# A block-causal mask in the softmax instead of in the products, and three moves around it

## The chip, the cores and the metric

The kernel runs on one core of one Trainium2 chip. The metric is the time of one execution in microseconds, as the device reports it; lower is better. Abbreviations as in the profile: PE is TensorE's matrix multiplication, PEld its weight load, ACT is ScalarE, DVE is VectorE, POOL is GpSimd, SP is SyncE, which here only issues DMAs.

## What is computed

An encoder trunk of two layers on 256 rows of 1024 columns, all in float32. Layer 0 is feed-forward, convolution, feed-forward; layer 1 is feed-forward, attention, feed-forward. The change touches the attention (8 heads; 128 columns of a query or key without rotation, 64 with it; chunks of 64 rows):

```python
chunk_id = jnp.arange(seq) // CHUNK                    # CHUNK = 64, seq = 256
for blk in range(seq // Q_BLOCK):                      # Q_BLOCK = 128
    q0, q1 = blk * Q_BLOCK, (blk + 1) * Q_BLOCK
    s = (jnp.einsum("bqhd,bkhd->bhqk", q_nope[:, q0:q1], k_nope[:, :q1], ...)
         + jnp.einsum("bqhr,bkr->bhqk", q_rope[:, q0:q1], k_rope[:, :q1], ...)) * scale
    mask = chunk_id[q0:q1, None] >= chunk_id[None, :q1]
    s = jnp.where(mask[None, None], s, -jnp.inf)
    p = jax.nn.softmax(s, axis=-1).astype(v.dtype)
    outs.append(jnp.einsum("bhqk,bkhd->bqhd", p, v[:, :q1]))
o = jnp.concatenate(outs, axis=1)
return o.reshape(o.shape[0], seq, N_HEADS * V_HEAD) @ w_o
```

A row sees its own chunk and the chunks before it. Of a block of 128 query rows the upper 64 therefore do not see the last 64 of the block's key columns, and the lower 64 see all of them.

## The kernel before, in words

All large products are made from two parts of each operand, a rounded high part and the rest, as three products (`mm3`, lines 269, 272 and 273). Weights come in blocks of 1 MB: SP's DMA into a `raw` tile (3 buffers), a cast to the high part on ACT (line 185), and the low part on DVE (line 186), each in two pieces, into `hi` and `lo` tiles (5 buffers). `load_to(n)` records the casts of all blocks up to number n; `load_ahead(k)` does so up to k blocks beyond the one in use.

A scheduler that works on the recorded program sets the final order of each engine. It follows the order of recording and the data, but instructions recorded under `urgent` have priority, and `order(a, b)` makes a follow b. `urgent` also keeps the last instructions of what it ran, and the casts recorded later are put behind these (`behind`).

The attention's products up to keys and values come first (`nope`, the copies at lines 1212 and 1257). The last weights of the queries, those of heads 4 to 7, are used after the first scores. Then, per head:

- `scores`: for each of two query blocks `qb`, a float32 product of the unrotated parts (line 1267), one of the rotated parts (line 1268), and a bfloat16 product of one row of ones with one row of -1e30 (line 1269), which adds -1e30 at the upper 64 rows and last 64 columns. Both blocks of a head, 128 and 256 columns, lie in one bank of the tag "B", of which there are 3.
- `softmax`: on DVE the maximum of each block (line 1279) and its scaling (line 1280); on ACT Exp with the sum of its row (line 1282, followed by a read of the accumulator); on DVE the reciprocal (line 1284) and the scaled probabilities (line 1286).
- `probs`: three transposes on PE (line 313, the same banks "B"), and a copy of the result, `ptT`, on ACT (line 1292).
- `values`: two float32 products with the values (lines 1301 and 1302), in one bank of the tag "C"; `evicted` copies the result to a high part `Oh` on ACT (line 1296) and a low part `Ol` on DVE (line 1297).
- the output projection, `Rows`: one block of weights for every two heads, 24 products of 512 columns.

The loop over `i` runs these staggered: the scores of head i, the transposes of head i-2, the values of head i-3, and at i = 6 and i = 8 a block of the projection. The other two blocks come in `finish`, which then adds to the residual rows and begins the next norm.

Of the kernel before, what the change touches and what calls it, by code (L numbers as in the profile page):

```python
# [11 lines left out]
F32 = mybir.dt.float32  # L12
F32R = mybir.dt.float32r
BF16 = mybir.dt.bfloat16
I32 = mybir.dt.int32
AF = mybir.ActivationFunctionType
ALU = mybir.AluOpType
AX = mybir.AxisListType

P = 128  # L20
D = 1024
S = 256
NT = S // P
# [4 lines left out]
CHUNK = 64  # L28
# [3 lines left out]
H = 8  # L32
# [10 lines left out]
PIECES = 2  # L43
# [16 lines left out]
SCALE = float((NOPE + ROPE) ** -0.5)  # L60
# [22 lines left out]
def trunk(ctx: ExitStack, tc: tile.TileContext, x, xt, pos, invf, gains, gfin, wdw,  # L83
          f1w13, f1w2, f2w13, f2w2, cw1, cw2, wa, wuq, wukv, wo, wpair, out):
    nc = tc.nc

    const = ctx.enter_context(tc.tile_pool(name="const", bufs=1))
# [4 lines left out]
    small = ctx.enter_context(tc.tile_pool(name="small", bufs=4))  # L92
# [5 lines left out]
    def uid(s):  # L98
        n_uid[0] += 1
        return f"{s}_{n_uid[0]}"  # L100
# [4 lines left out]
    def bank(tag, name):  # L105
        return ps.tile([P, 512], F32, tag=tag, name=uid(name), bufs=BANKS[tag])
# [23 lines left out]
    loaded = []  # L130
    n_used = [0]
# [3 lines left out]
    def order(ins, first):  # L135
        tc.add_manual_dep(ins.ins, first.name, mybir.DependencyInfo(
            mybir.DependencyClass.NoSync, mybir.DependencyReason.DATA), reason="order")
# [7 lines left out]
    casts = {}  # L145
# [13 lines left out]
    def load(src, pieces=1):  # L159
        if isinstance(src, tuple):  # L160
            raw = rawp.tile([P, HB], F32, tag="raw", name=uid("raw"))
            nc.sync.dma_start(raw, src[1])
            return raw
        n = src.shape[-1]
        there = len(loaded) in raws
        raw = raws.pop(len(loaded))[0] if there else rawp.tile([P, HB], F32, tag="raw", name=uid("raw"))
        hi = wp.tile([P, HB], F32R, tag="hi", name=uid("hi"))
        lo = wp.tile([P, HB], F32R, tag="lo", name=uid("lo"))
        if there:
            pass  # L170
        elif len(loaded) < 7:

            for i in range(pieces if len(loaded) < 4 else 1):
                c = slice(i * n // pieces, (i + 1) * n // pieces) if len(loaded) < 4 else slice(n)
                fetch(raw[:, c], src[:, c])
        else:
            dma = nc.sync.dma_start(raw[:, :n], src)
            if turns:

                order(dma, turns[-1].ins)  # L180
        for i in range(pieces):
            c = slice(i * n // pieces, (i + 1) * n // pieces)

            low = nc.gpsimd if len(loaded) == conv_block[-4] else nc.vector
            casts[len(loaded), i] = (nc.scalar.copy(hi[:, c], raw[:, c]),  # L185
                                     low.tensor_sub(lo[:, c], raw[:, c], hi[:, c].bitcast(F32)))  # L186
            for cast in casts[len(loaded), i]:
                behind(cast)
        return hi, lo
# [14 lines left out]
    def load_ahead(ahead=W_BUFS - 2):  # L204
        load_to(min(len(blocks), n_used[0] + ahead))

    def load_to(last):
        while len(loaded) < last:
            loaded.append(load(blocks[len(loaded)], PIECES))
# [29 lines left out]
    for k in range(KT):  # L239
        c = slice(k % 4 * 512, k % 4 * 512 + 512)  # L240
# [6 lines left out]
    neghalf = const.tile([P, 1], F32, name="neghalf")  # L247
# [19 lines left out]
    def mm3(o, ah, al, bh, bl, start, stop, after=()):  # L267

        mm = nc.tensor.matmul(o, ah, bl, start=start, stop=False)  # L269
        for a in after:  # L270
            order(mm, a.ins)
        nc.tensor.matmul(o, ah, bh, start=False, stop=False)  # L272
        return nc.tensor.matmul(o, al, bh, start=False, stop=stop)  # L273
# [8 lines left out]
    def tbs(tb):  # L282
        return slice(tb * P, (tb + 1) * P)
# [831 lines left out]
    def mla_in(act, X, make_next, cc, sn):  # L1115
        R = X.r
        CQ = act.tile([P, H, S], F32R, tag="CQ", name="CQ")
        CQh, CQl = CQ[:, :4, :], CQ[:, 4:, :]
# [4 lines left out]
        KR = act.tile([P, 2, S], F32, tag="KR", name="KR")  # L1123
        nc.gpsimd.memset(KR, 0.0)

        mq = const.tile([P, P], BF16, name="mq")
        nc.gpsimd.memset(mq, 0.0)
        nc.gpsimd.memset(mq[0:1, :CHUNK], 1.0)
        mk = const.tile([P, CHUNK], BF16, name="mk")
        nc.gpsimd.memset(mk, 0.0)  # L1130
        nc.gpsimd.memset(mk[0:1, :], -1e30)

        last_low = [None]

# [39 lines left out]
        last = None  # L1174
        for tb in range(NT):
# [5 lines left out]
            last = last_low[0]  # L1181
# [15 lines left out]
        QR = act.tile([P, 4, S], F32, tag="QR", name="QR")  # L1197
        KN = xp.tile([P, H, S], F32, tag="Xh", name="KN")
        QN = xp.tile([P, H, S], F32, tag="Xl", name="QN")
        VV = act.tile([P, NT, H * VH], F32, tag="VV", name="VV")  # L1200

        def nope(part, dst, nk, ch, cl, width, h0, heads, after=()):

            hi, lo = part
            for i in range(heads[0], heads[1], 2):
                b = bank("A", "nope")
                for e in range(2):
                    for k in range(nk):
                        c = slice(k * width + (i + e) * P, k * width + (i + e + 1) * P)
                        mm = mm3(b[:, e * S:(e + 1) * S], hi[:, c], lo[:, c], ch[:, k, :], cl[:, k, :],  # L1210
                                 k == 0, k == nk - 1, after if k == 0 else ())
                nc.scalar.copy(dst[:, h0 + i:h0 + i + 2, :], b.rearrange("p (e t) -> p e t", t=S))
            return mm
# [4 lines left out]
        for tb in range(NT):  # L1218
            u = bank("A", "qr")
            qu.append(u)  # L1220
            for k in range(4):
                after = (last,) if k == 0 else turned if (tb, k) == (0, 2) else ()
                last = mm3(u, CQh[:, k, tbs(tb)], CQl[:, k, tbs(tb)], hi[:, k * 512:(k + 1) * 512],
                           lo[:, k * 512:(k + 1) * 512], k == 0, k == 3, after)
# [13 lines left out]
        part, = weights()  # L1238
        last = nope(part, QN, 4, CQh, CQl, 512, 0, (0, 4), turned)
        for t in range(NT):  # L1240
            b = transposed(kd[t], 0, 1, (last,))
# [3 lines left out]
        for tb in range(NT):  # L1245
            b = transposed(qr[tb], 0, 4, (last,))
# [4 lines left out]
        for tb in range(NT):  # L1251
            for d in range(2):
                b = bank("A", "v")
                for k in range(2):
                    c = slice(k * D + d * 512, k * D + d * 512 + 512)
# [6 lines left out]
        def scores(hd):  # L1262
            b = bank("B", "sc")
            sc = {0: b[:, :P], 1: b[:, P:P + S]}
            for qb in range(NT):
                n = (qb + 1) * P
                nc.tensor.matmul(sc[qb], QN[:, hd, tbs(qb)], KN[:, hd, :n], start=True, stop=False)
                nc.tensor.matmul(sc[qb], QR[:, hd // 2, tbs(qb)], KR[:, hd % 2, :n], start=False, stop=False)
                nc.tensor.matmul(sc[qb][:, n - CHUNK:n], mq, mk, start=False, stop=True)
            return softmax(sc)  # L1270

        @urgent
        def softmax(sc):
            nm = small.tile([P, NT], F32, tag="nm", name=uid("nm"))
            sm = small.tile([P, NT], F32, tag="sm", name=uid("sm"))
            pr = act.tile([P, 3 * P], F32, tag="pr", name=uid("pr"), bufs=3)
            pn = {0: pr[:, :P], 1: pr[:, P:]}
            for qb in range(NT):
                nc.vector.reduce_max(nm[:, qb:qb + 1], sc[qb], axis=AX.X)
            nc.vector.tensor_scalar(nm, nm, -SCALE, None, op0=ALU.mult)  # L1280
            for qb in range(NT):
                nc.scalar.activation(pn[qb], sc[qb], AF.Exp, scale=SCALE, bias=nm[:, qb:qb + 1],
                                     accum_out=sm[:, qb:qb + 1])
            nc.vector.reciprocal(sm, sm)
            for qb in range(NT):
                nc.vector.tensor_scalar(pn[qb], pn[qb], sm[:, qb:qb + 1], None, op0=ALU.mult)
            return pr

        def probs(pr):
            b = transposed(pr, 0, 3)  # L1290
            pt = act.tile([P, 3 * P], F32, tag="ptT", name=uid("ptT"), bufs=2)
            nc.scalar.copy(pt, b[:, :3 * P])
            return pt
# [5 lines left out]
        def values(hd, pt):  # L1299
            b = bank("C", "pv")  # L1300
            nc.tensor.matmul(b[:, :S], VV[:, 0, hd * VH:(hd + 1) * VH], pt[:, :S], start=True, stop=False)
            nc.tensor.matmul(b[:, P:S], VV[:, 1, hd * VH:(hd + 1) * VH], pt[:, S:], start=False, stop=True)

            (urgent if hd in (3, 4) else lambda f: f)(evicted)(hd, b)

        pr, pt = {}, {}
        part, = weights()
        load_ahead(4)
        pr[0] = scores(0)
        nope(part, QN, 4, CQh, CQl, 512, 4, (0, 2))  # L1310
        pr[1] = scores(1)
        nope(part, QN, 4, CQh, CQl, 512, 4, (2, 4))
        o = Rows(Oh, Ol, H)
        for i in range(2, H + 3):
            if i < H:
                pr[i] = scores(i)
            if i == 6:
                load_ahead(5)
            if i - 2 < H:
                pt[i - 2] = probs(pr[i - 2])  # L1320
            if i - 3 in pt:
                values(i - 3, pt[i - 3])
            if i in (6, 8):
                o.block((i - 6) // 2)
        return o.finish(None, make_next, act)

    dw = const.tile([P, KT, TAPS], F32, name="dw")
# [137 lines left out]
```

## Time and profile before

| | |
|---|---|
| median of 3 runs | 923.6 us (923.42 to 923.61) |
| the profiled execution's own time | 923.93 us |
| its span (first to last instruction) | 922.1 us |
| granted TensorE clock | 0.999 of full speed |
| busy: PE, DVE, ACT, POOL | 911.7, 591.3, 494.6, 123.8 us |
| the attention from its first scores to the next norm's first transposes | 685.7 to 735 us of the span |

A row of the profile by time has the start, the time from the first start to the last end, the engine, the line, the operation with the tiles it writes and reads, and how many it merges; in square brackets, how long the engine sat idle before it and what ended that. Instructions overlap at their ends, so what an instruction costs its engine is the time from its start to the next start, not its length. A float32 product is two rows, since PE makes two passes of it. A group's row (line, engine, operation, shapes, count) has the busy time, the mean length in ns, and the idle time before.

### The profile page before, as it was taken

The page shows a single profiled execution, that of the slowest core. Times are in us where ns is not written, and L with a number is a line of the kernel's source. Part 1 is how long each engine was busy: PE and PEld are TensorE (multiplying, and loading weights), DVE is VectorE, ACT ScalarE, POOL GpSimd, SP SyncE. Part 2 cuts the span into 40 slices and gives each one's busy share as a digit, 9 for nine tenths or more (in the row PEclk, how much of TensorE's full clock was granted, in tenths as well). Part 3 has the DMA queues.
Part 4 walks back from the last instruction along what each step waited for, and adds up shares of the span by engine and source line. Part 5 has one row for each costly group of instructions (what it writes and reads, how often), then busy time and mean ns, then how long its engine had stood idle before and what let it go on. Part 6 is the DMA issues. An engine that isn't in the chain of part 4 may idle for free.

```text
span 922.1 us, 12110 instructions
## 1 busy us (share of the span) xinstructions
PE 911.7 (99%) x4348; PEld 764.8 (83%) x4348; DVE 591.3 (64%) x931; ACT 494.6 (54%) x844; POOL 123.8 (13%) x255
## 2 busy tenths in 40 slices
PE   9999999999999999999999999999999999999997
PEld 7888888898978888888888888888898788888886
DVE  6886664489987666664476665545785586556633
ACT  7655453488877444553365444533685474454422
POOL 1730000079942000000010000000200000000000
PEclk9999999999999999999999999999999999999999
DMA  9887775534217766775567776753471377677611
GB/s 332 313 300 254 279 250 220 183 138 137 93 61 272 261 229 234 252 253 197 183 223 265 245 245 233 253 187 132 171 278 50 138 260 275 234 244 261 224 46 46
DMA packets 65293, 194.73 MB, mean 211 GB/s; under 512 B 11857, under 2 KB 37073, under 8 KB 45905
## 3 DMA queue, kind: packets, MB, share of 16 engines
q1 hardware_dynamic: 64656, 193.27, 60.1%
q8 instruction: 34, 0.56, 0.2%
q10 hardware_dynamic: 576, 0.69, 0.2%
q14 instruction: 27, 0.21, 0.1%
HBM read 179.78 MB, written 14.16 MB: 210 GB/s over the span
## 4 chain that ended last, share of the span: by engine, by line
PE 96%; ACT 2%; DVE 1%; DMA 0%; issue 0%; POOL 0%; POOLq 0%; ACTq 0%; DVEq 0%
PE u L269 17%; PE u L272 17%; PE u L273 17%; PE o L269 9%; PE o L272 9%; PE o L273 9%; PE gate L744 3%; PE u L744 3%; PE o L993 1%; PE u L278 1%; PE tp L313 1%; PE pairs L787 1%; PE a L273 1%; PE a L269 1%; PE a L272 1%; PE nope L269 1%
## 5 line engine op out<-in xcount | busy, mean ns | idle before, releaser
L186 DVE TENSOR_TENSOR lo<-raw,hi 128x1024 fp32r<-128x1024 f32 (+1 forms) x292 | 344.4, 1220 | 187.4 <-ACT hi L185 186.8
L185 ACT CAST hi<-raw 128x1024 fp32r<-128x1024 f32 x294 | 292.8, 1048 | 254.8 <-PE o L273 89.6
L269 PE MATMUL u<-lo,Xh 128*128 128x512 f32 x688 | 267.9, 389 | 0.0
L273 PE MATMUL u<-hi,Xl 128*128 128x512 f32 x688 | 267.8, 389 | 0.0
L272 PE MATMUL u<-hi,Xh 128*128 128x512 f32 x688 | 267.7, 389 | 0.0
L273 PEld LDWEIGHTS u<-hi,Xl 128*128 128x128 f32 x688 | 129.2, 188 | 27.3 <-DVE Xl L332 0.4
L269 PEld LDWEIGHTS u<-lo,Xh 128*128 128x128 f32 x688 | 129.2, 188 | 27.2 <-DVE lo L186 0.4
L272 PEld LDWEIGHTS u<-hi,Xh 128*128 128x128 f32 x688 | 129.2, 188 | 26.6
L272 PE MATMUL o<-hi,Gh 128*128 128x512 f32 (+1 forms) x356 | 137.9, 387 | 0.0
L273 PE MATMUL o<-hi,Gl 128*128 128x512 f32 (+1 forms) x356 | 137.8, 387 | 0.0
L269 PE MATMUL o<-lo,Gh 128*128 128x512 f32 (+1 forms) x356 | 137.2, 387 | 0.0
L304 POOL TENSOR_TENSOR ms<-ss 128x1 f32<-128x1 f32 x16 | 8.0, 504 | 597.7 <-ACT junk L296 597.7
L269 PEld LDWEIGHTS o<-lo,Gh 128*128 128x128 f32 x356 | 66.9, 188 | 13.6
L273 PEld LDWEIGHTS o<-hi,Gl 128*128 128x128 f32 x356 | 66.9, 188 | 13.5
L272 PEld LDWEIGHTS o<-hi,Gh 128*128 128x128 f32 x356 | 66.9, 188 | 13.3
L637 DVE TENSOR_TENSOR Gl<-gb,Gh 128x512 fp32r<-128x512 f32 (+1 forms) x48 | 31.4, 653 | 48.1 <-ACT Gh L636 48.1
L636 ACT CAST Gh<-gb 128x512 fp32r<-128x512 f32 (+1 forms) x48 | 28.0, 583 | 60.5 <-DMA gb<-gd 60.5
L821 DVE SCALAR_TENSOR_TENSOR acc<-V,dw,acc 128x128 f32<-128x128 f32 (+1 forms) x176 | 54.5, 395 | 0.0
L842 ACT ACTIVATE prod<-V,dw 128x128 f32<-128x128 f32 (+1 forms) x129 | 46.0, 415 | 1.8 <-POOL Y L843 1.0
L712 DVE TENSOR_TENSOR s<-s,u 128x512 f32<-128x512 f32 (+1 forms) x48 | 30.5, 636 | 8.1 <-PE u L273 8.1
L711 ACT ACTIVATE s<-u,R 128x512 f32<-128x512 f32 (+1 forms) x48 | 31.2, 650 | 5.6 <-PE u L273 4.6
L345 DVE STREAM_TRANSPOSE gt<-s 128x512 f32<-128x512 f32 (+1 forms) x48 | 32.0, 666 | 1.5
(213 smaller groups left out, 860.6 us busy)
## 6 DMA issues: line engine op xcount, KB each, us to landing
raw<-in_f2w SPq DMA_DIRECT2D x66, 1024.0 KB, 4.9
raw<-in_f1w SPq DMA_DIRECT2D x62, 1024.0 KB, 5.0
raw<-in_cw SPq DMA_DIRECT2D x12, 1024.0 KB, 4.7
gd<-gt SPq DMA_DIRECT2D x160, 64.0 KB, 3.4
gb<-gd SPq DMA_DIRECT2D x40, 256.0 KB, 4.3
raw<-in_wo SPq DMA_DIRECT2D x4, 1024.0 KB, 4.8
raw<-in_wuq SPq DMA_DIRECT2D x3, 1024.0 KB, 4.7
raw<-in_f1w SPq DMA_DIRECT2D x8, 256.0 KB, 5.6
```

What stands on the lines that cost most here:

```text
L185: casts[len(loaded), i] = (nc.scalar.copy(hi[:, c], raw[:, c]), low.tensor_sub(lo[:, c], raw[:, c], hi[:, c].bitcast(F32)))
L186: low.tensor_sub(lo[:, c], raw[:, c], hi[:, c].bitcast(F32)))
L269: mm = nc.tensor.matmul(o, ah, bl, start=start, stop=False)
L272: nc.tensor.matmul(o, ah, bh, start=False, stop=False)
L273: return nc.tensor.matmul(o, al, bh, start=False, stop=stop)
L345: nc.vector.transpose(t[:, :w], src.rearrange("p (t j q) -> p j t q", t=n, q=32))
L637: nc.vector.tensor_sub(Gl[:, f, tbs(tb)].rearrange("p t (i q) -> p t i q", q=32), bv, gh.bitcast(F32))
L711: nc.scalar.activation(s[:, :w], u[0, tb][:, :w], AF.Silu, scale=X.r[tb])
L712: nc.vector.tensor_mul(s[:, :w], s[:, :w], u[0, tb][:, w:] if both else u[1, tb])
L744: mm = nc.tensor.matmul(u[:, t], w[:, c], X.x[:, k, t], start=(k == 0), stop=(k == KT - 1))
L821: dve_last.append(nc.vector.scalar_tensor_tensor(out if j == j1 - 1 else y, v, w, y, op0=ALU.mult, op1=ALU.add))
L842: prods_last.append(nc.scalar.activation(p, v, AF.Copy, scale=w))
```

## The change

- The bfloat16 products of the mask go, and so do their two operands `mq` and `mk`. The softmax works on ranges of 64 rows instead: for each of a head's four ranges the maximum, the Exp and the row sums run over just the columns that the range sees, 64, 128, 192 and 256 of them. The probabilities that the mask excludes are never written; the three tiles that hold probabilities are now fixed (`PR`), and POOL stores zeros in these places once.
- The scores of head 2 are recorded ahead of the queries of heads 6 and 7, and the first product of each group of late queries is put behind the last product of the scores recorded so far.
- Exp's table is loaded by an Exp of one column that is put behind the last cast recorded so far.
- The evictions of heads 5 and 6 become `urgent`, as those of heads 3 and 4 are, and the casts of the next weights are recorded by one block at i = 8 and one at i = 9.

```diff
-        mq = const.tile([P, P], BF16, name="mq")
-        nc.gpsimd.memset(mq, 0.0)
-        nc.gpsimd.memset(mq[0:1, :CHUNK], 1.0)
-        mk = const.tile([P, CHUNK], BF16, name="mk")
-        nc.gpsimd.memset(mk, 0.0)
-        nc.gpsimd.memset(mk[0:1, :], -1e30)
+        PR = [act.tile([P, 3 * P], F32, tag=f"pr{i}", name=uid("pr")) for i in range(3)]
+        for pr in PR:
+            for c in (P, 3 * P):
+                nc.gpsimd.memset(pr[:CHUNK, c - CHUNK:c], 0.0)
...
-                nc.tensor.matmul(sc[qb], QR[:, hd // 2, tbs(qb)], KR[:, hd % 2, :n], start=False, stop=False)
-                nc.tensor.matmul(sc[qb][:, n - CHUNK:n], mq, mk, start=False, stop=True)
-            return softmax(sc)
+                last = nc.tensor.matmul(sc[qb], QR[:, hd // 2, tbs(qb)], KR[:, hd % 2, :n], start=False, stop=True)
+            score_last.append(last)
+            return softmax(hd, sc)
...
-            pr = act.tile([P, 3 * P], F32, tag="pr", name=uid("pr"), bufs=3)
+            pr = PR[hd % 3]
...
-            for qb in range(NT):
-                nc.vector.reduce_max(nm[:, qb:qb + 1], sc[qb], axis=AX.X)
+            seen = [(qb, slice(i * CHUNK, (i + 1) * CHUNK), qb * P + (i + 1) * CHUNK) for qb in range(NT)
+                    for i in range(P // CHUNK)]
+            for qb, r, n in seen:
+                nc.vector.reduce_max(nm[r, qb:qb + 1], sc[qb][r, :n], axis=AX.X)
             nc.vector.tensor_scalar(nm, nm, -SCALE, None, op0=ALU.mult)
-            for qb in range(NT):
-                nc.scalar.activation(pn[qb], sc[qb], AF.Exp, scale=SCALE, bias=nm[:, qb:qb + 1],
-                                     accum_out=sm[:, qb:qb + 1])
+            for qb, r, n in seen:
+                nc.scalar.activation(pn[qb][r, :n], sc[qb][r, :n], AF.Exp, scale=SCALE, bias=nm[r, qb:qb + 1],
+                                     accum_out=sm[r, qb:qb + 1])
...
-            (urgent if hd in (3, 4) else lambda f: f)(evicted)(hd, b)
+            (urgent if hd in (3, 4, 5, 6) else lambda f: f)(evicted)(hd, b)
...
+        table = nc.scalar.activation(small.tile([P, 1], F32, tag="silu", name="exp"), neghalf, AF.Exp)
+        order(table, casts[len(loaded) - 1, PIECES - 1][0].ins)
         pr[0] = scores(0)
-        nope(part, QN, 4, CQh, CQl, 512, 4, (0, 2))
+        nope(part, QN, 4, CQh, CQl, 512, 4, (0, 2), score_last[-1:])
         pr[1] = scores(1)
-        nope(part, QN, 4, CQh, CQl, 512, 4, (2, 4))
+        pr[2] = scores(2)
+        nope(part, QN, 4, CQh, CQl, 512, 4, (2, 4), score_last[-1:])
         o = Rows(Oh, Ol, H)
         for i in range(2, H + 3):
-            if i < H:
+            if 2 < i < H:
                 pr[i] = scores(i)
...
+            if i in (8, 9):
+                load_to(n_used[0] + i - 4)
```

More of the change, by code (lines that the diff above doesn't have):

```diff
@@ L1267, in scores, with softmax @@
                 nc.tensor.matmul(sc[qb], QN[:, hd, tbs(qb)], KN[:, hd, :n], start=True, stop=False)
-                nc.tensor.matmul(sc[qb], QR[:, hd // 2, tbs(qb)], KR[:, hd % 2, :n], start=False, stop=False)
-                nc.tensor.matmul(sc[qb][:, n - CHUNK:n], mq, mk, start=False, stop=True)
-            return softmax(sc)
+                last = nc.tensor.matmul(sc[qb], QR[:, hd // 2, tbs(qb)], KR[:, hd % 2, :n], start=False, stop=True)
+            score_last.append(last)
+            return softmax(hd, sc)
         @urgent
-        def softmax(sc):
+        def softmax(hd, sc):
             nm = small.tile([P, NT], F32, tag="nm", name=uid("nm"))
             sm = small.tile([P, NT], F32, tag="sm", name=uid("sm"))
-            pr = act.tile([P, 3 * P], F32, tag="pr", name=uid("pr"), bufs=3)
+            pr = PR[hd % 3]
             pn = {0: pr[:, :P], 1: pr[:, P:]}
-            for qb in range(NT):
-                nc.vector.reduce_max(nm[:, qb:qb + 1], sc[qb], axis=AX.X)
+            seen = [(qb, slice(i * CHUNK, (i + 1) * CHUNK), qb * P + (i + 1) * CHUNK) for qb in range(NT)
+                    for i in range(P // CHUNK)]
+            for qb, r, n in seen:
+                nc.vector.reduce_max(nm[r, qb:qb + 1], sc[qb][r, :n], axis=AX.X)
             nc.vector.tensor_scalar(nm, nm, -SCALE, None, op0=ALU.mult)
-            for qb in range(NT):
-                nc.scalar.activation(pn[qb], sc[qb], AF.Exp, scale=SCALE, bias=nm[:, qb:qb + 1],
-                                     accum_out=sm[:, qb:qb + 1])
+            for qb, r, n in seen:
+                nc.scalar.activation(pn[qb][r, :n], sc[qb][r, :n], AF.Exp, scale=SCALE, bias=nm[r, qb:qb + 1],
+                                     accum_out=sm[r, qb:qb + 1])
             nc.vector.reciprocal(sm, sm)
@@ L1302, in values @@
             nc.tensor.matmul(b[:, P:S], VV[:, 1, hd * VH:(hd + 1) * VH], pt[:, S:], start=False, stop=True)
-            (urgent if hd in (3, 4) else lambda f: f)(evicted)(hd, b)
-        pr, pt = {}, {}
+            (urgent if hd in (3, 4, 5, 6) else lambda f: f)(evicted)(hd, b)
+        pr, pt, score_last = {}, {}, []
         part, = weights()
         load_ahead(4)
+        table = nc.scalar.activation(small.tile([P, 1], F32, tag="silu", name="exp"), neghalf, AF.Exp)
+        order(table, casts[len(loaded) - 1, PIECES - 1][0].ins)
         pr[0] = scores(0)
-        nope(part, QN, 4, CQh, CQl, 512, 4, (0, 2))
+        nope(part, QN, 4, CQh, CQl, 512, 4, (0, 2), score_last[-1:])
         pr[1] = scores(1)
-        nope(part, QN, 4, CQh, CQl, 512, 4, (2, 4))
+        pr[2] = scores(2)
+        nope(part, QN, 4, CQh, CQl, 512, 4, (2, 4), score_last[-1:])
         o = Rows(Oh, Ol, H)
         for i in range(2, H + 3):
-            if i < H:
+            if 2 < i < H:
                 pr[i] = scores(i)
```

## The prediction

> **What bounds the kernel now.** I read the page's first and fourth parts, then the busy time by stage, the waits of TensorE (PE), and the attention stage (685 to 735 us of the span) in order of time, engine by engine.
>
> ```profile
> span 922.1 us, 12110 instructions
> PE 911.7 (99%) x4348; PEld 764.8 (83%) x4348; DVE 591.3 (64%) x931; ACT 494.6 (54%) x844; POOL 123.8 (13%) x255
> PE 96%; ACT 2%; DVE 1%; DMA 0%; issue 0%; POOL 0%; POOLq 0%; ACTq 0%; DVEq 0%
> 685.00:700.00 15.00, 14.89 (x109) 13.55 (x108) 8.87 (x25) 10.31 (x27) 0.00 (x0) 1.00 0.55 207
> 720.00:740.00 20.00, 19.42 (x92) 15.43 (x91) 13.25 (x23) 12.08 (x27) 1.15 (x4) 1.00 0.34 122
> PE o L269 <- ACT Oh L1296: 0.6, 1, 0.6
> ```
>
> PE is busy 99% of the span and is 96% of the chain that ended last, so whatever takes products off PE shortens the end, unless PE then waits instead. The two stage rows (columns: busy time of PE, weight loads, DVE, ACT, POOL; the clock granted; DMA) say how little there is to win here beside the products: PE is idle 0.11 us in the first stage and 0.58 us in the second, at full clock. The row of the waits names the second: PE waits for head 5's output, which ACT copies.
>
> The built program of the changed kernel has the same instructions in the same order as before on all engines up to the first scores, and again after the attention's last head; SP's queue, with all the weights' DMAs, is in the same order throughout. Only PE, ACT and DVE between 685 and 735 us differ, and POOL, below. So I price that stretch alone.
>
> **1. The mask products leave PE.** Sixteen bf16 products (two for each of 8 heads).
>
> ```profile
> 690.27 0.39 PE L1268 MATMUL sc<-KR,QR 128*128 128x128 f32 x2
> 690.50 0.19 PE L1269 MATMUL sc<-mk,mq 128*128 128x64 bf16 x1
> 690.53 0.68 PE L1267 MATMUL sc<-KN,QN 128*128 128x256 f32 x2
> 691.04 0.59 PE L1268 MATMUL sc<-KR,QR 128*128 128x256 f32 x2
> 691.47 0.19 PE L1269 MATMUL sc<-mk,mq 128*128 128x64 bf16 x1
> 691.50 0.36 PE L269 MATMUL nope<-CQ,hi 128*128 128x256 f32 x1
> 691.70 0.28 PE L272 MATMUL nope<-CQ,hi 128*128 128x256 f32 x1
> 691.83 0.28 PE L273 MATMUL nope<-CQ,lo 128*128 128x256 f32 x1
> ```
>
> PE is pipelined, so the price is from start to start. A mask takes 0.03 us itself (690.50 to 690.53). But the product behind it is late: the 256-column pair after a mask takes 0.51 us (690.53 to 691.04), the same size without one before it 0.43 (691.04 to 691.47); a nope product after a mask 0.20, else 0.13 or less. So each mask costs 0.11 us. Before a transpose it is less:
>
> ```profile
> 700.54 0.19 PE L1269 MATMUL sc<-mk,mq 128*128 128x64 bf16 x1
> 700.74 0.36 PE tp L313 x3
> 705.59 0.33 PE tp L313 x3
> ```
>
> The last two rows, of the chain by time, are three transposes behind a mask and behind other products: 0.03 us more, and 0.03 for the mask itself, 0.06 us. All 8 first masks stand before a 256-column pair (0.88 us); of the second ones 3 stand before other products (0.33) and 5 before transposes (0.30). Sum: **-1.5 us** on the path.
>
> **2. Two waits of PE go.**
>
> ```profile
> 697.70 0.19 PE L1269 MATMUL sc<-mk,mq 128*128 128x64 bf16 x1
> 698.00 0.55 PE L313 MATMUL tp<-ident,pr 128*128 128x128 f32 x3
> 720.68 3.90 ACT L185 CAST hi<-raw 128x1024 fp32r<-128x1024 f32 x4
> 724.48 0.38 ACT L1296 CAST Oh<-pv 128x256 fp32r<-128x256 f32 x1
> 724.74 0.50 ACT L1292 COPY ptT<-tp 128x384 f32<-128x384 f32 x1
> 724.91 0.50 PE L269 MATMUL o<-lo,Oh 128*128 128x512 f32 x1 [0.58 <-ACT Oh L1296]
> 725.24 0.40 PE L272 MATMUL o<-hi,Oh 128*128 128x512 f32 x1
> 725.48 0.39 PE L269 MATMUL o<-lo,Oh 128*128 128x512 f32 x1
> ```
>
> At 697.70 the next start should be 0.03 later and is 0.30 later: 0.27 us for a bank of scores that ACT still reads. At 724.9 PE waits for Oh, whose copy stands behind four casts. The row shows 0.58 us idle after the modelled end of the product before. A product is modelled 0.39 long and the next starts after 0.24 (725.48 row, and 725.24 to 725.48), so from start to start it is 0.58 + 0.15 = 0.73; and the product that ended the wait takes 0.33 instead of 0.24 (724.91 to 725.24): 0.1 for weights loaded late. I add that 0.1 to every wait, old or new. The two are 0.37 + 0.83 = **-1.2 us**. In the new order Oh of head 5 stands ahead of the casts, and each later one has two casts at most before it and 3.4 us of PE work in which to be made: nothing is late there.
>
> **3. What takes their place.** Softmax by half tiles of 64 rows does 64+128+192+256 columns in four instructions, where 128+256 in two did before.
>
> ```profile
> 692.43 0.37 ACT L1282 ACTIVATE pr<-sc,nm 128x128 f32<-128x128 f32 x1 [0.31 <-DVE nm L1280]
> 692.70 0.19 ACT L1282 ACTIVATION_READ_ACCUMULATOR pr<-sc,nm 128x1 f32 x1
> 692.79 0.47 ACT L1282 ACTIVATE pr<-sc,nm 128x256 f32<-128x256 f32 x1
> 693.24 0.36 ACT L1282 ACTIVATE pr<-sc,nm 128x128 f32<-128x128 f32 x1
> 691.70 0.62 DVE L1279 TENSOR_REDUCE nm<-sc 128x1 f32<-128x128 f32 x2 [1.12 <-PE sc L1269]
> 692.24 0.29 DVE L1280 TENSOR_SCALAR nm<-nm 128x2 f32<-128x2 f32 x2
> L1279 DVE TENSOR_REDUCE nm<-sc 128x1 f32<-128x128 f32 x8 | 2.3, 285 | 4.8 <-PE sc L1269 4.8
> L1279 DVE TENSOR_REDUCE nm<-sc 128x1 f32<-128x256 f32 x8 | 3.3, 414 | 0.0
> L1292 ACT COPY ptT<-tp 128x384 f32<-128x384 f32 x8 | 3.9, 484 | 1.5 <-PE tp L313 1.5
> 685.62 1.10 ACT L1257 COPY VV<-v 128x512 f32<-128x512 f32 x2
> 687.70 2.36 DVE L186 TENSOR_TENSOR lo<-raw,hi 128x1024 fp32r<-128x1024 f32 x2 [0.99 <-ACT hi L185]
> 685.66 0.38 PE L1267 MATMUL sc<-KN,QN 128*128 128x128 f32 x2
> ```
>
> With its accumulator read an Exp takes 0.36 us for 128 columns (692.43 to 692.79) and 0.45 for 256 (692.79 to 693.24). No row has 64 or 192; on the same line they are 0.31 and 0.40 (estimates). A head goes from 0.81 to 1.52 us on ACT. The two maxima take 0.54 us (691.70 to 692.24): 0.21 and 0.33; on their line 64 and 192 columns take 0.14 and 0.27, so a head goes from 0.54 to 0.94 on DVE. Bounds: at worst 64 and 192 cost what 128 and 256 do (1.62 and 1.08); at best the 256 added columns cost only their slope (0.09 us for 128 on ACT, 0.12 on DVE), and two more accumulator reads 0.09 each (1.17 and 0.78). I take the line through the two rows of the same instruction.
>
> PE between start and start needs, without masks, 2x0.22 + 2x0.43 = 1.31 us for a head's scores, 0.33 for its transposes, 0.43 + 0.22 = 0.65 for its values (products of the same two sizes), 24x0.12 = 2.87 for two heads of late queries. On ACT a 512-column copy takes 0.48 (two are 1.10 with the last one's tail), ptT 0.38 before the next may start, Oh 0.26 (724.48 to 724.74); on DVE two low parts 2.3. With these I walked the queues of PE, ACT and DVE in the new program's order from the first scores, keeping every wait; the old program walked so gives the trace's two waits at 698.0 and 724.9 and no other above 0.1 us. The new one has five:
>
> - Head 1's Exp. DVE's order is now: maxima of head 1, maxima of head 2, then head 1's scaling of the maximum. Head 2's scores end at 685.66 + 3x1.31 + 2.87 = 692.46 us, plus 0.19 until DVE sees them; two maxima more and the scaling, and Exp 1 starts at 693.8. Exps 1 and 2 take 3.04, the copy of the late queries 0.48, then ptT of head 0: PE can use it at 697.87. PE itself is at 685.66 + 4x1.31 + 2x2.87 + 2x0.33 = 697.30, plus a short wait (0.06) for head 2's bank: so 0.06 and **0.43** late.
> - Head 5's scores need the bank that Exp 3 reads. Exp 3 starts at 698.8 (head 3's maxima, then head 2's probabilities come first on DVE) and ends at 700.4; PE comes at 700.26: **0.2**.
> - The first later casts. ACT takes two (1.9) right behind Exp 6, DVE their low parts (2.3), and head 7's maxima and Ol of head 2 stand behind these: values of head 4 wait **0.2** at 714.7. Exp 7 is late with them, and Oh of head 3 behind Exp 7: **0.35** at 716.7.
>
> Sum 1.24, and 0.1 for each of the five: **+1.7 us**. Not priced on the path: Exp's table load (1.28 us, row below), which now runs behind the last cast at 688.5, where ACT would else wait for the first maximum; the POOL stores of zeros (6, after KR's), in 7 us in which POOL idles, ahead of the first norm; the Pool wait on the transposes, long over by then.
>
> ```profile
> 690.84 1.28 ACT L1282 ACT_TABLE_LOAD   x1
> 642.86 0.53 POOL L1124 MEMSET KR<- 128x512 f32 x1 [3.71 <-DMA hd<-ht]
> 650.30 0.19 POOL L304 TENSOR_TENSOR ms<-ss 128x1 f32<-128x1 f32 x1 [6.92 <-ACT junk L296]
> ```
>
> The load's cover is head 0's slack of about 0.8 us; without it 0.3 us would appear at head 3's scores. From its start to the first Exp are 1.59 us (690.84 to 692.43), and the last 0.31 of these is a wait for DVE. The Trainium skill, "ScalarE: Activation LUTs", section "What ACT_TABLE_LOAD costs", puts a switch at 2.66 us, with a drain of 1.38; with that the sum would be -0.7. The trace has no room for such a drain, and I keep 1.28.
>
> **Sum.** -1.5 - 1.2 + 1.7 = **-1.0 us** on the profiled execution. Its time is 923.93 us, its span 922.1; the median of the runs is 923.6 (923.42 to 923.61), 0.3 below it. On that median: 922.6.
>
> **Rivals.**
> - *Softmax keeps up.* If half tiles of 64 rows cost only their columns (the lower bounds), the walk leaves one wait, 0.4 at 700.0, and gives -2.3, at 921.3; if no wait at all came, -2.7 (920.9). For: DVE is busy 8.87 and ACT 10.31 us of 15 in this stage. Against: fixed parts show in every pair of rows above. Chance 0.16.
> - *Nothing left of it.* At the upper bounds the waits grow to 0.2, 0.43, 0.34, 0.16, 0.3 and 0.44, and the walk ends at -0.1 (923.5). Chance 0.10.
> - *Slower: ACT becomes the bound from 693 us on.* A head then needs 1.52 + 0.38 (ptT) + 0.26 (Oh) = 2.16 us of ACT and 1.31 + 0.33 + 0.65 = 2.29 of PE. Where the half-tile Exps cost over 0.03 us more each than my line, ACT takes longer than PE for a head, and each score bank is freed later. With 0.04 more on each Exp and maximum the walk gives +0.4, with 0.08 +2.2, at 925.8. For: twice as many instructions read each bank, and the trace has none on 64 rows here; against: a half tile runs the same instruction as the rows above, whose price went with the columns. Chance 0.06. The Trainium skill, "Perfetto Trace Analysis", section "Optimizing Scalar/DVE Operations", advises larger instead of more operations where such an engine is saturated, for a fixed cost of each; by that rule this is the case to fear. The trace agrees that there is a fixed cost, but in no stage here is ACT full.
> - The mask's cost could have been hidden anyway; a PE idle for 0.11 us of 15 leaves no place for that.
>
> **Numbers.** The forecast has 0.68 (own range 921.9 to 923.3). A measurement of this kernel can tell about 0.2%, 1.85 us: faster is under 921.75, slower over 925.45. Faster: the first rival and a tail of the forecast, 0.18. Slower: 0.06. Same: 0.76. The range from 921.3 to 923.9 holds the forecast, the second rival and half of the first.
>
> **What would show it.** Right: no bf16 product in the attention; PE's wait for Oh at 724.9 gone; new waits of PE for ptT near 697.9, for a score bank near 700.5, for Oh near 716.7; stage 685 to 735 shorter by 1 us, every other stage as before; an Exp of 64 columns at about 0.32 us as the rows count it, and of 192 at 0.42. Wrong: waits of PE in that stage of over 2.5 us, 64-column Exps near 0.37, or a difference that arises before 685 or after 740 us.

## The result, and the profile after

| | before | changed |
|---|---|---|
| time, median of 6 runs each on one chip | 923.51 us (923.36 to 924.01) | 927.76 us (927.0 to 928.6) |
| ratio, 95% interval | | 1.0045 (1.0034 to 1.0055) |
| span of the profiled run | 922.1 us | 925.2 us |

The forecast was 922.6 us, in a range of 921.3 to 923.9. The changed kernel is 4.2 us slower than before: the range missed it, and the sign was wrong too. The busy times of the changed kernel's engines, from its page:

```profile
PE 911.4 (99%) x4332; PEld 764.3 (83%) x4332; DVE 596.7 (64%) x947; ACT 502.3 (54%) x877; POOL 123.4 (13%) x257
```

PE has 16 instructions fewer (4348 to 4332): the mask products are gone. ACT has 33 more and 7.7 us more of busy time, DVE 16 and 5.4. The busy time by stage, one row of before that was not shown yet, then three of the changed kernel:

```profile
700.00:720.00 20.00, 20.00 (x114) 16.97 (x113) 10.21 (x33) 8.68 (x28) 0.00 (x0) 1.00 0.14 53
```

```profile
685.00:700.00 15.00, 12.96 (x91) 11.63 (x90) 10.49 (x30) 12.07 (x35) 0.00 (x0) 1.00 0.52 191
700.00:720.00 20.00, 17.97 (x97) 14.74 (x96) 12.42 (x40) 13.48 (x47) 0.00 (x0) 1.00 0.12 43
720.00:740.00 20.00, 19.31 (x94) 15.72 (x94) 11.43 (x20) 10.43 (x25) 0.40 (x3) 1.00 0.33 119
```

PE was busy for 14.89, 20.00 and 19.42 us before and is for 12.96, 17.97 and 19.31 now, at the same full clock. The first two stages, which are the heads, lost about 2 us each. PE's rows with a wait, from the timeline of the changed kernel (in brackets the idle time before the row and what ended it):

```profile
696.31 0.49 PE L1266 MATMUL sc<-KN,QN 128*128 128x128 f32 x2 [1.16 <-ACT pr L1284]
698.34 0.52 PE L313 MATMUL tp<-ident,pr 128*128 128x128 f32 x3 [0.45 <-issue]
699.28 0.70 PE L1303 MATMUL pv<-ptT,VV 128*128 128x256 f32 x2 [0.43 <-ACT ptT L1294]
702.60 0.49 PE L1266 MATMUL sc<-KN,QN 128*128 128x128 f32 x2 [0.76 <-ACT pr L1284]
715.38 0.50 PE L269 MATMUL o<-lo,Oh 128*128 128x512 f32 x1 [0.76 <-ACT Oh L1298]
718.34 0.67 PE L1303 MATMUL pv<-ptT,VV 128*128 128x256 f32 x2 [0.51 <-DVE nm L1282]
720.84 0.50 PE L269 MATMUL o<-lo,Oh 128*128 128x512 f32 x1 [0.67 <-ACT Oh L1298]
```

Seven waits stand where the forecast had five. Their idle times add up to 4.74 us. The forecast counted from start to start, and by that measure each wait is 0.16 us longer: a transpose is modelled 0.27 us long while the next product starts after 0.11, and a 512-column product 0.39 while the next starts after 0.23. So the waits are 1.33, 0.62, 0.59, 0.93, 0.93, 0.67 and 0.84 us, 5.9 in all, against 1.24 in the forecast. Those at 698.34, 699.28, 702.60, 718.34 and 720.84 are the five of the forecast (0.06, 0.43, 0.2, 0.2 and 0.35), in its order and up to 4 us later, since each wait shifts the next; all five are longer. For the one at 698.34 the profile names no releaser; the last read of Exp's accumulator for head 2 ends 0.1 us before it. The waits at 696.31 (a bank that an Exp still reads) and 715.38 (Oh) are new. Why the waits are longer is in ACT's and DVE's rows for head 0 (some rows left out):

```profile
690.06 0.31 ACT L1284 ACTIVATE pr<-sc,nm 64x64 f32<-64x64 f32 x1 [0.65 <-DVE nm L1282]
690.27 0.19 ACT L1284 ACTIVATION_READ_ACCUMULATOR pr<-sc,nm 64x1 f32 x1
690.48 0.36 ACT L1284 ACTIVATE pr<-sc,nm 64x128 f32<-64x128 f32 x1
690.75 0.19 ACT L1284 ACTIVATION_READ_ACCUMULATOR pr<-sc,nm 64x1 f32 x1
690.96 0.42 ACT L1284 ACTIVATE pr<-sc,nm 64x192 f32<-64x192 f32 x1
...
692.08 0.58 ACT L1211 COPY QN<-nope 128x512 f32<-128x512 f32 x1
```

```profile
687.29 1.33 DVE L1281 TENSOR_REDUCE nm<-sc 64x1 f32<-64x64 f32 x4 [1.31 <-PE sc L1267]
688.66 1.23 DVE L186 TENSOR_TENSOR lo<-raw,hi 128x1024 fp32r<-128x1024 f32 x1
```

The durations are the forecast ones: 0.31 and 0.42 us for 64 and 192 columns, where 0.32 and 0.42 were expected. The spacing is not. Before, the next Exp started 0.09 us after the accumulator read began (692.70 to 692.79). Here it starts 0.20 to 0.22 after it (690.27 to 690.48, and so behind every Exp of the eight heads but one, where ACT waits for something else), so a read of 0.19 us runs to its end before the next instruction begins. A head takes 692.08 - 690.06 = 2.02 us of ACT instead of the 1.52 forecast, and 688.66 - 687.29 = 1.37 us of DVE instead of 0.94.

### The profile page after: what moved, and what is told of

Its sections match the earlier page's. It is cut to its first block, busy times and chain, and to the rows that moved or that the text cites. A ratio compares the mean times of both kernels' runs of the same rounds, so it can differ in the third digit from the quotient of the medians.

```text
span 925.2 us, 12135 instructions
## 1 busy us (share of the span) xinstructions
PE 911.4 (99%) x4332; PEld 764.3 (83%) x4332; DVE 596.7 (64%) x947; ACT 502.3 (54%) x877; POOL 123.4 (13%) x257
## 4 chain that ended last, share of the span: by engine, by line
PE 95%; DVE 2%; ACT 2%; issue 0%; POOL 0%; POOLq 0%; ACTq 0%; DVEq 0%
PE u L273 17%; PE u L269 17%; PE u L272 17%; PE o L269 9%; PE o L273 9%; PE o L272 9%; PE gate L744 3%; PE u L744 3%; PE o L993 1%; PE u L278 1%; ACT pr L1284 1%; PE tp L313 1%; DVE nm L1281 1%; PE pairs L787 1%; PE a L272 1%; PE a L269 1%
## 5 line engine op out<-in xcount | busy, mean ns | idle before, releaser
L843 POOL TENSOR_TENSOR odd<-odd,prod 128x128 f32<-128x128 f32 (+1 forms) x62 | 34.3, 558 | 0.0
```

The lines of the kernel that those rows point to most:

```text
L843: pool_last.append(nc.gpsimd.tensor_tensor(o, o, p, op=ALU.add))
```

## Theory and rivals

The walk of the three queues that gave the forecast, with these two spacings put in (0.12 us more on each Exp, the maxima 0.23, 0.31, 0.36 and 0.46 us apart) and nothing else changed, gives +3.2 us and seven waits at the places above, of 0.5 to 1.2 us from start to start. So the spacing was the theory, with three open questions. Does the time follow from the spacing, or from one of the moves? What makes the spacing: the change of half, the 64 rows, or the number of instructions with small outputs? And is there an order in which the ranges pay?

One column below is the time from the first row of scores on PE (684.90 us in the changed kernel, 685.66 before) to the end of the span, which leaves out what differs from run to run ahead of the stage.

```profile
684.90 0.39 PE L1266 MATMUL sc<-KN,QN 128*128 128x128 f32 x2
```

| kernel | median us | ratio to before, 95% interval | first scores to end, against before's 236.4 | walk |
|---|---|---|---|---|
| changed | 927.76 | 1.0045 (1.0034 to 1.0055) | +3.9 | +3.2 |
| e1 products back | 922.42 | 0.9989 (0.9981 to 0.9998) | -1.2 | -1.2 |
| e2 half order | 925.11 | 1.0017 (1.0008 to 1.0025) | +1.4 | +0.9 |
| e3 four full | 922.81 | 0.9991 (0.9983 to 1.0000) | -0.9 | -0.6 |
| e4 every second head | 921.80 | 0.9980 (0.9971 to 0.9989) | -1.9 | -1.9 |
| e5 third head not ahead | 923.20 | 0.9996 (0.9987 to 1.0005) | -0.6 | -0.8 |
| e6 ranges alone | 924.74 | 1.0010 (1.0001 to 1.0019) | +0.8 | +0.5 |
| e7 head 2 by product | 921.32 | 0.9974 (0.9964 to 0.9984) | -2.5 | -2.5 |

The kernel before took 923.57 us beside e1 to e4 and 923.72 beside e5 to e8. e3 and e8 leave out the mask and so compute another softmax; only their times are of use. The walks of e1 to e7 are the numbers in the expectations; that of the changed kernel was made with its own measured spacings.

## Experiments

**e1: the moves without the ranges.**

```diff
-  last = nc.tensor.matmul(sc[qb], QR[...], KR[...], start=False, stop=True)
+  nc.tensor.matmul(sc[qb], QR[...], KR[...], start=False, stop=False)
+  last = nc.tensor.matmul(sc[qb][:, n - CHUNK:n], mq, mk, start=False, stop=True)
...
-  for qb, r, n in seen:        # four ranges
+  for qb in range(NT):         # two blocks of 128 rows, maxima and Exps
```

> The changed kernel with the mask products and the softmax over 128 rows of the kernel before; every other move of the change stays (third head's scores ahead, table load early, Oh of heads 5 and 6 urgent, later casts early). Spacing theory (the loss is the half-tile Exps and maxima, which here start about 0.2 us after the accumulator read, or only at the end of the one before): no PE wait is left in 685 to 735 us, the old waits at 698.0 and 724.9 included; 1.1 to 1.2 us faster than before, 922.4, and over 5 us faster than the changed kernel. Rival, that one of the moves costs (order of the heads or the casts): the waits for scores, Oh and values stay and the time stays over 925.

Measured: 922.42 us, and no wait of PE between 684 and 745 us. The moves do what the second step of the prediction priced (1.2 us for the two old waits), and together they cost nothing with the softmax of before. The loss comes with the ranges.

**e2: the same four ranges, in another order.**

```diff
-  seen = [... for qb in range(NT) for i in range(P // CHUNK)]
+  seen = [... for i in range(P // CHUNK) for qb in range(NT)]
```

> The changed kernel with the four ranges of a head in another order: both of rows 0 to 63 first, then both of rows 64 to 127. Three theories of the lost overlap. If it is the change of the half from one instruction to the next that stops the overlap, an Exp on the same half starts 0.09 us after its predecessor's accumulator read and one on the other half 0.20 us after it, the maxima likewise (a 64-row maximum followed on the same half is 0.14 us to the next, not 0.23), and the time is 2.4 us below the changed kernel (+0.9 against before, 924.4). If every 64-row instruction runs without overlap, all spacings stay at 0.20 and the time at 927.8. If it is the many instructions into one small tile, the same 927.8; the third run tells these two apart.

Measured: 925.11 us, 2.65 below the changed kernel's median. From its timeline on ACT, head 0 (rows 0 to 63 in the first two Exps, 64 to 127 in the last two):

```profile
690.36 0.31 ACT L1284 ACTIVATE pr<-sc,nm 64x64 f32<-64x64 f32 x1 [0.48 <-DVE nm L1282]
690.57 0.19 ACT L1284 ACTIVATION_READ_ACCUMULATOR pr<-sc,nm 64x1 f32 x1
690.67 0.40 ACT L1284 ACTIVATE pr<-sc,nm 64x192 f32<-64x192 f32 x1
690.97 0.19 ACT L1284 ACTIVATION_READ_ACCUMULATOR pr<-sc,nm 64x1 f32 x1
691.19 0.36 ACT L1284 ACTIVATE pr<-sc,nm 64x128 f32<-64x128 f32 x1
...
692.12 0.59 ACT L1211 COPY QN<-nope 128x512 f32<-128x512 f32 x1
```

On the same half the next Exp starts 0.09 to 0.10 us after the read (690.57 to 690.67), on the other half 0.21 to 0.22 (690.97 to 691.19). The pair on rows 64 to 127 is 0.09 apart as well, so it is not the upper half that is slow. A head takes 1.76 us instead of 2.02 with the same instructions. Of the three theories only the change of half fits; that every 64-row instruction runs alone is ruled out. The time is 0.7 us above the 924.4 expected: the same seven waits remain, 3.5 us from start to start.

**e3: four instructions on all 128 rows.**

```diff
-  nc.vector.reduce_max(nm[r, qb:qb + 1], sc[qb][r, :n], axis=AX.X)
+  nc.vector.reduce_max(nm[:, c:c + 1], sc[qb][:, :n], axis=AX.X)
...
-  nc.scalar.activation(pn[qb][r, :n], sc[qb][r, :n], AF.Exp, ...)
+  to = pn[qb] if c % 2 else JUNK[:, 32 * c:32 * c + n]
+  nc.scalar.activation(to, sc[qb][:, :n], AF.Exp, ...)
```

> The changed kernel with four maxima and four Exps for each head of the same 64, 128, 192 and 256 columns, but on all 128 rows (the mask is left out: rows 0 to 63 keep the 64 masked keys; the narrow results go to a spare tile and to sums of their own). If the half tile (64 rows) is what costs, the spacing goes back to 0.09 us after each accumulator read and the maxima to 0.14, 0.21, 0.27 and 0.33 us, PE's waits are about as forecast for the change (0.43 for ptT, 0.3 for a bank, 0.5 for Oh) and the time is 0.6 us below before, 922.9. If it is the number of instructions or their small outputs, the spacing stays at 0.20 and the time near 926.5 to 927.8.

Measured: 922.81 us. Its rows on ACT, first and last of head 0:

```profile
690.26 0.32 ACT L1286 ACTIVATE junkp<-sc,nm 128x64 f32<-128x64 f32 x1
...
691.75 0.60 ACT L1213 COPY QN<-nope 128x512 f32<-128x512 f32 x1
```

The same four column counts take 1.49 us for a head on ACT, where the forecast had 1.52, and 688.93 - 687.99 = 0.94 on DVE, as forecast. So neither the number of instructions nor their small outputs cost more than the line through the old rows said.

The kernel also comes close to the prediction's own walk put to a run, since its instructions cost what the line said, and the forecast waits are there. Only one is long enough for the profile to mark it:

```profile
697.82 0.70 PE L1305 MATMUL pv<-ptT,VV 128*128 128x256 f32 x2 [0.29 <-ACT ptT L1296]
699.89 0.49 PE L313 MATMUL tp<-ident,pr 128*128 128x128 f32 x3
700.43 0.49 PE L1268 MATMUL sc<-KN,QN 128*128 128x128 f32 x2
714.21 0.49 PE L313 MATMUL tp<-ident,pr 128*128 128x128 f32 x3
714.78 0.67 PE L1305 MATMUL pv<-ptT,VV 128*128 128x256 f32 x2
```

Three transposes take 0.33 us to the next start; here they take 0.54 (699.89 to 700.43) and 0.57 (714.21 to 714.78), so 0.21 and 0.24 us are waits. From start to start PE loses 0.10 us at 697.01 for head 2's bank, 0.45 at 697.82 for ptT, 0.21 at 700.43 for a bank, 0.24 at 714.78 for the values and 0.30 at 716.74 for Oh. The prediction had 0.06, 0.43, 0.2, 0.2 and 0.35 at these places, and -1.0 us where e3 has -0.9 from the first scores on. (The walk made for e3, in its expectation, had 0.3 for the bank, 0.5 for Oh and -0.6.)

**e8: 64 rows and 128 rows in turn, all from row 0.** An edit of e3, for the spacing alone (maxima and sums in fixed tiles).

```diff
+  r = slice(0, P) if c % 2 else slice(0, CHUNK)
-  nc.scalar.activation(to, sc[qb][:, :n], AF.Exp, ...)
+  nc.scalar.activation(to[r], sc[qb][r, :n], AF.Exp, ...)
```

> Spacing only; mask left out. The four-instruction kernel over all 128 rows with the narrow Exps and maxima (64 and 192 columns) on rows 0 to 63 alone, to a spare tile, and the wide ones (128 and 256) on all 128 rows: the number of rows changes at each instruction, the first row is always 0. If a change of the first row is what stops the overlap, an Exp starts 0.09 us after the read before it, and the maxima are 0.14, 0.20, 0.27 and 0.33 us apart as on 128 rows. If any change of the range of rows does it, 0.20 and 0.23 to 0.46.

Measured, in one execution: 922.80 us. Head 0 on ACT and on DVE:

```profile
690.17 0.31 ACT L1292 ACTIVATE junkp<-sc,nms 64x64 f32<-64x64 f32 x1 [0.17 <-DVE nms L1288]
690.38 0.19 ACT L1292 ACTIVATION_READ_ACCUMULATOR junkp<-sc,nms 64x1 f32 x1
690.47 0.35 ACT L1292 ACTIVATE pr<-sc,nms 128x128 f32<-128x128 f32 x1
...
691.66 0.58 ACT L1217 COPY QN<-nope 128x512 f32<-128x512 f32 x1
```

```profile
687.91 1.01 DVE L1287 TENSOR_REDUCE nms<-sc 64x1 f32<-64x64 f32 x4 [1.33 <-PE sc L1273]
688.85 1.21 DVE L186 TENSOR_TENSOR lo<-raw,hi 128x1024 fp32r<-128x1024 f32 x1
```

A change from 64 to 128 rows with the same first row keeps the overlap: 0.09 us after the read (690.38 to 690.47), 1.49 us for a head on ACT and 688.85 - 687.91 = 0.94 on DVE, the forecast 0.94. What stops the overlap, on both engines, is that an instruction starts on another row than the one before it. Which of its operands must do so (the scores, the probabilities, the maxima or the sums) was not separated; here all change together.

For DVE the Trainium skill has this as a rule, which the prediction did not use: "VectorE: DVE Perf Modes", section "Two Vector instructions with no wait between them", says, as a model, that a Vector instruction is held until all earlier ones have finished if an input starts in another group of 32 partitions than the first input of the last instruction that read that memory, or its output in another than the last output into that memory. The runs agree: 1.37 us for a head's four maxima where each changes the first row, 0.94 in e8 where none does. With the maxima alone at that price the walk gives +1.1 us, an estimate that no run shows. The ACT rows above show the same on ScalarE.

**e4: ranges in every second head.**

```diff
+  if hd in (0, 2, 4, 6):       # mask by product
+      last = nc.tensor.matmul(sc[qb][:, n - CHUNK:n], mq, mk, start=False, stop=True)
...
+  if hd in (0, 2, 4, 6):       # softmax over 128 rows
+      seen = [(qb, slice(0, P), (qb + 1) * P) for qb in range(NT)]
```

> The changed kernel with heads 0, 2, 4 and 6 masked by products (softmax over 128 rows, as before) and heads 1, 3, 5 and 7 by ranges. Spacing theory: ACT has time to catch up in every second head, so no wait of PE over 0.05 us comes, 8 mask products are off PE (about 0.75 us), and the two old waits are gone (1.2): 1.9 us faster than before, 921.6. Rival, that one head by ranges already delays what PE needs next: four waits of 0.2 to 0.4, about 922.5 to 923.5.

Measured: 921.80 us and no wait of PE in the stage. Four heads by ranges cost PE nothing when ACT has four cheap ones between them.

**e5: the ranges without one of the moves.**

```diff
   pr[1] = scores(1)
-  pr[2] = scores(2)
   nope(part, QN, 4, CQh, CQl, 512, 4, (2, 4), score_last[-1:])
...
-  if 2 < i < H:
+  if i < H:
       pr[i] = scores(i)
```

> The changed kernel with one move undone: the third head's scores stand behind the last queries again, where the kernel before has them; ranges, early table load and early casts stay. With the spacings measured in the changed kernel (0.12 us more for each Exp whose successor starts on another half, maxima 0.23, 0.31, 0.36 and 0.46 apart) the walk of the queues gives the changed kernel as it was measured (+3.2 us against before, seven waits of PE at their places), and this one at -0.8, 922.8: Oh of each head then stands ahead of the next head's Exps on ACT, and one wait of PE is left, 1.8 us for a bank of scores near 700 us. So the slow spacing would cost only together with the order of the heads. Rival, that the spacing costs by itself, whatever the order: 926 to 927.5.

Measured: 923.20 us, no different from before, with all eight heads by ranges and every Exp at the slow spacing. PE's one wait, then ACT's order near 700 us here, then in the changed kernel:

```profile
699.63 0.49 PE L1266 MATMUL sc<-KN,QN 128*128 128x128 f32 x2 [1.78 <-ACT pr L1284]
```

```profile
699.60 0.48 ACT L1294 COPY ptT<-tp 128x384 f32<-128x384 f32 x1
699.98 0.38 ACT L1298 CAST Oh<-pv 128x256 fp32r<-128x256 f32 x1
700.38 0.31 ACT L1284 ACTIVATE pr<-sc,nm 64x64 f32<-64x64 f32 x1
```

```profile
698.26 0.58 ACT L1211 COPY QN<-nope 128x512 f32<-128x512 f32 x1
698.74 0.87 ACT L1294 COPY ptT<-tp 128x384 f32<-128x384 f32 x2
700.55 0.31 ACT L1284 ACTIVATE pr<-sc,nm 64x64 f32<-64x64 f32 x1 [0.94 <-DVE nm L1282]
...
702.58 0.37 ACT L1298 CAST Oh<-pv 128x256 fp32r<-128x256 f32 x1
```

With the third head's scores ahead, the Exps of heads 1 and 2 follow each other, the last copy of the late queries and ptT stand behind both, and Oh stands behind the next head's Exps. In e5 Oh stands ahead of them. The ranges are not free in e5 either: its one wait is 1.95 us from start to start and takes back most of what the mask products and the old waits had cost (2.7). But the move that was free in e1 costs over 4 us here. That ACT's order carries this is read from the rows; the edit changes the order of the scores on PE as well.

**e6: the kernel before with the ranges alone.** The diff is the softmax and the mask products of the change, without its other edits.

> The kernel before with the ranges alone (mask products gone, softmax by half tiles), and none of the moves. Walk with the measured spacings: the 1.5 us of mask products are given back in three waits of PE, 0.8 for scores near 696, 1.8 for scores near 700.6 and 0.4 for Oh near 725: +0.5 us, 924.1. Rival, that the ranges carry the whole loss: 927 or more.

Measured: 924.74 us. Its waits of PE:

```profile
696.52 0.49 PE L1266 MATMUL sc<-KN,QN 128*128 128x128 f32 x2 [0.64 <-ACT pr L1282]
700.73 0.49 PE L1266 MATMUL sc<-KN,QN 128*128 128x128 f32 x2 [1.63 <-ACT pr L1282]
725.70 0.50 PE L269 MATMUL o<-lo,Oh 128*128 128x512 f32 x1 [0.35 <-ACT Oh L1296]
```

All three are at the places expected, and from start to start they are 0.81, 1.80 and 0.51 us, where 0.8, 1.8 and 0.4 were expected. Ranges alone cost 1.0 us by the medians and the moves alone save 1.15 (e1); together they cost 4.2. The two parts of the change work against each other.

**e7: a version that beats both.** The order of e2, and the condition of e4 with head 2 alone.

```diff
+  if hd in (2,):               # mask by product, softmax over 128 rows
...
-  seen = [... for qb in range(NT) for i in range(P // CHUNK)]
+  seen = [... for i in range(P // CHUNK) for qb in range(NT)]
```

> A version to beat both: the changed kernel with head 2 alone masked by products (its Exps and maxima over 128 rows), the other seven by ranges, and for these both ranges of rows 0 to 63 first. Walk: ACT has the 1.2 us of head 2 back where heads 0 to 2 crowd, no wait of PE is left between 685 and 735 us, 14 mask products are off PE and the two old waits gone: -2.5 us, 921.1. Rival, that seven heads by ranges keep ACT behind: the waits for Oh near 714 to 721 stay, 922.5 or more.

Measured: 921.32 us, 0.9974 of before (0.9964 to 0.9984). Its busy time by stage:

```profile
685.00:700.00 15.00, 15.00 (x108) 14.07 (x107) 11.24 (x36) 12.92 (x40) 0.00 (x0) 1.00 0.54 199
700.00:720.00 20.00, 20.00 (x108) 17.06 (x107) 11.86 (x39) 12.67 (x45) 0.00 (x0) 1.00 0.15 53
720.00:740.00 20.00, 20.00 (x95) 16.35 (x95) 14.74 (x25) 12.79 (x29) 3.03 (x8) 1.00 0.44 145
```

PE is not idle in any of the three. With the order of e2, one head of eight with cheap Exps, at the place where three heads crowd ACT, is enough; the other seven keep their mask products off PE.

## Why the prediction was wrong

**Step 1, the mask products: right.** e1 and e7 both run without waits and differ by 14 products; 14/16 of 1.5 us is 1.3, and they differ by 1.3 us from the first scores on (1.25 by the medians, each against before). e1 and e4 differ by 8 products and 0.7 us, where half of 1.5 is 0.75. The products are on the path, so the rival of a hidden mask falls.

**Step 2, the two old waits: right.** e1 has neither and gains 1.2 us. The table load was where it was put, 1.28 us long, and hidden: ACT still waits 0.65 us for DVE before head 0's first Exp. The load starts at 687.91, and ACT's next instruction at 689.21, 0.02 us after its end, so nothing further is paid behind it.

**Step 3, what takes their place: this step failed, in one term, the price of a head's maxima and Exps.** The line through 128 and 256 columns gave 1.52 us of ACT and 0.94 of DVE for a head. e3 and e8 measure 1.49 and 0.94 for exactly these column counts, so the line was right, for instructions that start on one row. The changed kernel alternates between rows 0 and 64, which the line did not know of, and pays 2.02 and 1.37. With that term put right, the same walk gives +3.2 us instead of -1.0. The queues and the waits were right: where the line's price holds, in e3, all five waits come at their places and within 0.05 us of their sizes. Of the prediction's signs of being wrong the long waits came, and the longer Exp (near 0.37 us for 64 columns) did not: the price lies in the spacing, not in the duration of 0.31. Its bounds failed for the same reason: the upper one, 1.62 us, let 64 and 192 columns cost what 128 and 256 do, and still assumed the overlap. (The six waits at these bounds add up to 1.87 us, 2.47 with 0.1 for each, which makes -0.2 and not the -0.1 written there; nothing else hangs on it.)

**The rival "ACT becomes the bound" was the nearest to what happened, and 0.06 was too little for it.** It noted that the trace has no such instruction on 64 rows, and against it stood only that a half tile runs the same instruction, whose price went with the columns. The trace has no such Exp, but it has copies, at 64 rows in alternating halves, which the prediction passed over. The groups of before and its timeline on ACT:

```profile
L1244 ACT COPY KR<-tp 64x128 f32<-64x128 f32 x4 | 1.0, 260 | 0.0
```

```profile
673.92 1.07 ACT L1244 COPY KR<-tp 64x128 f32<-64x128 f32 x4
675.02 2.00 ACT L185 CAST hi<-raw 128x1024 fp32r<-128x1024 f32 x2
```

Four copies of 0.26 us each take 675.02 - 673.92 = 1.10 us, 0.275 apiece: none starts before the one ahead of it has ended. The Oh copy of 128 rows and twice the columns is 0.38 us long and lets the next start after 0.26. The missing 0.1 us per instruction could have been read there, and at 0.08 to 0.12 the prediction's own walk stood at +2.2 and above.

Two things of that rival did not hold. ACT and DVE both pay, and which of them costs more was not separated on the chip. And ACT is no bound from 693 us on whatever the order: at the same 2.02 us for a head e5 has one wait of PE instead of seven and is no slower than before. How much of it PE sees depends on the order.

**What stays open.** Kernels without waits (e1, e4, e7) agree with the walk within 0.1 us; the changed kernel and e2, with seven waits each, are 0.7 and 0.5 above it, e6 with three 0.3. The 0.1 us added for each wait is not at fault: in the changed kernel the product behind a wait comes 0.08 to 0.11 us late at six of the seven, 0.6 us in all, and 5.9 + 0.6 - 2.7 = +3.8 us against +3.9 measured. So it is the waits themselves that the walk has too short, by about 0.7 us together, and why was not found. Nor was it found what makes the time at which PE reaches the first scores differ by up to 1.6 us between profiled runs (684.90 in the changed kernel, 686.46 in e4).

## What to carry to other kernels

Price an instruction by the distance to its successor, and look whether the instruction that this distance is taken from starts on the same row of its tile as its neighbours, and whether the one to be priced will; a duration or a slope over columns does not tell it. When an instruction on ACT or DVE is split by rows as here, do all pieces that start on one row before those that start on another. And price the parts of a change together: a reordering that is free while an engine has slack can cost several times what the work that fills this slack costs alone (here over 4 us, against 1.0 for the ranges alone).

## What the hardware showed that was not expected

- On ACT the overlap of one instruction with the next (0.12 us here, an Exp behind an accumulator read) is lost whenever the first row changes between 0 and 64, in either direction, and kept when only the number of rows changes (0.20 to 0.22 us from the read to the next instruction against 0.09, wherever ACT waits for nothing else in the changed kernel, e2 and e8).
- On DVE the four maxima of a head take 1.37 us with a change of first row at each, 688.96 - 687.80 = 1.16 in the order of e2 and 0.94 without one:

```profile
687.80 1.13 DVE L1281 TENSOR_REDUCE nm<-sc 64x1 f32<-64x64 f32 x4 [1.34 <-PE sc L1267]
688.96 1.23 DVE L186 TENSOR_TENSOR lo<-raw,hi 128x1024 fp32r<-128x1024 f32 x1
```

- On ACT and DVE, instructions of 64 and 192 columns on 128 rows cost no more than the line through those of 128 and 256 (e3: 1.49 us for a head against 1.52 on ACT, 0.94 against 0.94 on DVE).
